# Layer 1 attention of a two-block kernel: score products issued as a set, the query norm's factor taken into the softmax, other order estimates

## The chip, the core and the metric

The kernel runs on one core of one Trainium2 chip. The metric is the device time of one execution in microseconds (us), taken as the median of repeated runs. The engines of the core are named as in the profile: PE is TensorE (PEld its weight loads), DVE is VectorE, ACT is ScalarE, POOL is GpSimd and SP is SyncE, which here issues the loads.

## What is computed

Two transformer blocks follow each other on 256 tokens of 1024 features, in float32. The first has dilated attention, a state-space part and a gated feed-forward. The second has two layers with a modulation from a conditioning vector: layer 0 is a convolution module on two streams (the latent x and a context), layer 1 is grouped-query attention of x over both streams. The change is in layer 1; this is its part of the reference, cut to what matters:

```python
def gqa_project(h, w_qkv, q_norm, k_norm):
    ...   # 16 query heads, 4 key heads, 64 wide
    return rms_norm(q, q_norm), rms_norm(k, k_norm), v

def softmax_attend(q, k, v):
    s = jnp.einsum('bkgqd,bkld->bkgql', q, k).astype(jnp.float32) * (q.shape[-1] ** -0.5)
    p = jax.nn.softmax(s, axis=-1).astype(v.dtype)
    return jnp.einsum('bkgql,bkld->bkgqd', p, v)

def gqa_mixer(hl, hc, w_qkv, q_norm, k_norm, w_o, tables, with_ctx):
    ...
    ql = apply_axial_rope(ql, tables)
    kl = apply_axial_rope(kl, tables)
    k_all = jnp.concatenate([kc, kl], axis=2)      # 512 keys
    ...
    ol = merge_heads(blocked_attend(ql, k_all, v_all)) @ w_o
```

`rms_norm` divides a head's 64 values by the root of their mean square and multiplies by a gain per value.

## The kernel before

**Recording and ordering.** The program does not issue its instructions as it goes. `Recorder.add` notes each of them with the tiles that it reads and writes and with a cost in nanoseconds from `Recorder.cost`. `Recorder.schedule` then plays the engines against each other with these costs: an engine that is free takes, of the instructions whose inputs are ready and whose tiles have room, the one that comes first in the program. The result is one fixed order for each engine, and that is what runs. So a changed cost moves instructions in the whole program, not only where the change was made. `together` puts several products into one entry of that list, so that nothing comes between them.

**Products in three passes.** Weights and activations are split into a high and a low part (names with h and l: `gh`, `gl`, `hqkv`, `lqkv`), and each product runs as low x high, high x high, high x low. ACT makes the high part, DVE the low one.

**Layer 1 attention.** `q_proj` computes eight tiles of two query heads each (products `pq`, 24 per tile, copied to `qf`) and their squares' sums (`hsq`); after four tiles `HeadNorm.done` works out 1/rms on [128 tokens, 16] tiles (`hn`, a chain of ten small DVE instructions). `q_norm(j)` calls `HeadNorm.apply`: four PE products `hb` (each shows as two records) spread the factor over the partitions, DVE multiplies `qf` by gain and factor (`ht`), then come the rotation (a shuffle, two products with the tables `cos2` and `sin2`, a sum) and the split to `q1h`, `q1l`. Keys go through the same function to `k1h`, `k1l`.

For each pair of heads j (8) and half of the queries i (2), called a unit below (16 units), there are two heads side by side. The scores of a head are three products `S` that use 64 of the array's 128 rows (form 64\*128 in the trace); the two heads sit in the two halves of the rows and can run side by side. DVE takes the row maximum (`am`), ACT the exponential (`P`, with its sum `dn`), DVE scales by 1/sum. PE transposes P in four pieces a head (`pt`, form 128\*128), ACT copies them (`PT`), and eight products `po` (form 128\*64, together in one set) give the output, split to `o1h`, `o1l`. The output projection `pw` follows; some of it runs between the units. Scores of the first half go to PSUM banks of tag `at`, those of the second to `py` and `sb`; transposes and `hb` share the bank `ax`, and from the second pair on one head's transposes use `md`.

**Other stages that the order touches.** The modulation of layer 0 is 24 groups of four products `pm` of form 128\*32, spread as fillers over the first part of the program. The state-space part ends in eight sets of products `py`, which need DVE's tiles `DF`. In the convolution of the latent stream DVE works through 152 taps (`lcv`); a chain of mean (`mul`), square sums (`sslb`), a small norm (`pclb`, `bclb`) and DVE's `lsl` ends in the products `p<-lsl`. The context's products there read `csl` and `csh`.

Of the kernel before, what the change touches and what calls it, by code (L numbers as in the profile page):

```python
# [21 lines left out]
T = 256  # L22
# [7 lines left out]
# ---------------------------------------------------------------------------  # L30
# Weight streams: each stream is a list of chunks; a chunk is [128, w] in SBUF.
# ---------------------------------------------------------------------------
# [21 lines left out]
# columns of the parameter pack  # L54
# [3 lines left out]
def _prm(spec):  # L58
# [9 lines left out]
    ("wdw", 248), ("bdw", 8), ("lng", 8), ("lnb", 8), ("gq", 1), ("gk", 1),  # L68
# [30 lines left out]
HURRY, C2, CS_TAG = 4, 2, "S"  # L99
UC = ("sE", "sE", "sw", "sw")  # L100
# [5 lines left out]
# ---------------------------------------------------------------------------  # L106
# Recording of the kernel's instructions, and a list scheduler that orders them.
# ---------------------------------------------------------------------------
def _rearranged(a, pattern, sizes):
    # numpy form of AP.rearrange for the few patterns used here  # L110
# [21 lines left out]
class View:  # L132
    """A part of a virtual tile: `ix` are the elements that it covers, in quadrants of 32 partitions."""
# [47 lines left out]
class Op:  # L181
    __slots__ = ("n", "eng", "calls", "outs", "deps", "cost", "lat", "prio", "succ", "wait", "reserve",
                 "tiles", "start", "end", "pos", "cols", "urgent", "begun", "ready")


class Section:
    """Instructions that `spread` sets between others of the program."""
# [17 lines left out]
class Recorder:  # L205
# [18 lines left out]
    @contextmanager  # L224
    def together(self, rounds):
        # instructions of one engine that stay together: products in column tiles that run side by side
        self.set = []
        yield
        parts, self.set = self.set, None
        op = parts[0]  # L230
        op.deps = sorted({d for o in parts for d in o.deps})
        op.calls = [c for o in parts for c in o.calls]
        op.outs = [v for o in parts for v in o.outs]
        op.tiles = list({id(t): t for o in parts for t in o.tiles}.values())
        one = max(o.cost for o in parts)
        op.cost = rounds * one + 25.0 * (len(parts) - rounds)
        op.cols = rounds * one * 2.4
        self.ops.append(op)
        self.prio += 1.0

    def add(self, eng, fn, args, kw):
# [36 lines left out]
        op.cost, op.lat = self.cost(eng, fn, args, kw, ins, outs)  # L278
        if eng == "tensor":
            op.cols = (op.cost - 2.5) * 2.4 * min(1.0, args[1].shape[0] / 128)  # L280
# [8 lines left out]
    def cost(self, eng, fn, args, kw, ins, outs):  # L289
        """Nanoseconds that an instruction holds its engine, and until others see its result."""  # L290
# [5 lines left out]
        if eng == "tensor":  # L296
            moving = args[2] if fn == "matmul" else args[1]
            n = math.prod(moving.shape[1:]) if fn == "matmul" else 128
            f32 = args[1].dt == FT
# [10 lines left out]
        if fn == "tensor_tensor_scan":  # L310
            return 100 + 1.042 * n, 140.0
# [15 lines left out]
    def schedule(self):  # L327
        """Orders the instructions: each engine takes, when it is free, the ready one that comes first in the program
        and whose tiles fit. Tiles are taken early only where all that comes before still fits."""
# [10 lines left out]
        # room left in each tag along the program  # L340
# [22 lines left out]
        columns = {}  # L363
        soon = {e: [] for e in engines}
        while done < len(ops):
            progress = False
            for e in engines:
# [39 lines left out]
                if e == "tensor":  # L407
                    # the array runs at half its rate until one tick of its clock's monitor was busy
                    tick_ = int(now / HAM_TICK)
                    if columns.get(tick_ - 1, 0.0) < HAM_COLUMNS:  # L410
                        cost = max(25.0, 2 * (cost - 2.5))
                    n = pick.cols
# [19 lines left out]
            while future and future[0][0] <= now:  # L432
                _, kind, _, n = heapq.heappop(future)
                op = ops[n]
                # its own engine sees a result at once, the others after `lat`
# [32 lines left out]
def two_blocks(ctx: ExitStack, tc: tile.TileContext, I, out):  # L468
# [15 lines left out]
    def held(mark):  # L484
        # not before the instruction of that mark
# [21 lines left out]
    class Feat:  # L507
        # n feature tiles of w columns each, in pieces of 4 KiB (tag S) or 3 KiB (tag Q)
# [100 lines left out]
    def rsqrt(v, y, t, h):  # L609
        # y = 1/sqrt(v) for v > 0: a guess from the bits, and a polynomial of v guess^2  # L610
# [12 lines left out]
    class Norm:  # L623
        # 1 / rms over the features of [128, 8, T] tiles; broadcast over partitions
# [16 lines left out]
        def column(self, pc):  # L641
            # the mean square of each token, tokens on partitions
# [14 lines left out]
    def spread_rows(y, n, name, tag="ax"):  # L657
        # [128 tokens, 2 n] -> [128, n, T], the same on every partition
# [8 lines left out]
    def two_rstd(n1, n2):  # L667
        # n1 for x, n2 for g x: 1 / rms(x) and its product with 1 / rms(g x / rms(x))
# [68 lines left out]
    # ======================= block 1 =========================================  # L737
# [25 lines left out]
    # SSM parameters and rotary tables of block 1  # L763
# [4 lines left out]
    ssc = const("ssc", [128, 16, 16], FT)  # small SSM vectors  # L768
# [8 lines left out]
    def prelude():  # L777
# [13 lines left out]
        # rotary tables: [token, (quadrant, half, freq)] transposed to [dim, token]  # L791
# [10 lines left out]
        # z = (abar - 1) / lambda  # L802
# [15 lines left out]
        # c' = c z  # L818
# [17 lines left out]
    # u = n @ w_in[u]  # L836
# [17 lines left out]
    def cmul(oc, os, ac, as_, bc_, bs, shape, name):  # L854
        # (oc + i os) = (ac + i as)(bc + i bs)
# [9 lines left out]
    def ssm():  # L865
        # tables e^{i theta t}, t = 16 a + b, from A[b] and B[a]
        # the rotation starts anew at each half of the sequence
        H = T // 2
        tabs = slot("tabs", [128, 2, 2, 16, 16])  # (cos/sin, A/B, n, state tile)
# [10 lines left out]
        for q in range(4):  # L880
            py = bank("py", (128, T), "py")
            E = [rec.tile("sE", [128, 4, 8, 16], FT, "E") for _ in range(2)]  # cos/sin: (state tile, a, b)
# [5 lines left out]
            for s2 in range(2):  # L888
                DF = []
                for s in (2 * s2, 2 * s2 + 1):  # L890
# [19 lines left out]
                    for h in range(2):  # L910
                        if h:
                            # the state in the new frame: e^{i theta 128} g
# [13 lines left out]
                # y = c're (D_re - F_im) - c'im (F_re + D_im)  # L926
# [52 lines left out]
    def mod_part(parts):  # L979
        # sixths of layer 1's modulation for a stream each: weighted on the vector engine, summed over partitions  # L980
        # on the tensor engine
# [32 lines left out]
    # chunks of the modulation: 0 shift1, 8 scale1, 16 gate1, 24 shift2, 32 scale2, 40 gate2  # L1014
    def modulated(x, gain, bias, bc, put, name):
        # put(k) -> (hi, lo) destinations
# [25 lines left out]
    def conv_front(hx, s, name, on_pe, tg, stag, ntag="ax"):  # L1042
        # convolution module from its modulated input up to the last product's operand
        st = Stream("pw1")
        acc = Feat(name + "cv")
        for j in range(8):
# [10 lines left out]
            # some taps as products with diagonal matrices, the others on the vector engine  # L1057
# [17 lines left out]
        # layer norm over features  # L1075
# [26 lines left out]
    def do_mods(groups, a, b):  # L1102
        # these groups of the modulation, between places a and b of the program
# [14 lines left out]
    def slot_proj(j):  # L1118
# [27 lines left out]
        vv = slot("vv", [128, 2, 384], FT, "Q")  # (token block, 3 heads x 128)  # L1146
# [4 lines left out]
    def slot_attn(j, q_, k_, vv):  # L1151
        sp = bank("sp", (128, 2, T), "at")  # scores of the third group, and the output
        po = sp[:, 1]
        for i in range(2):
# [20 lines left out]
            pt = slot("PT", [128, 3, nk], FT, "Q")  # (group, (key block, query))  # L1175
# [33 lines left out]
    def table(fn, mark):  # L1209
        # loads the tables of a function ahead of its first use  # L1210
# [561 lines left out]
```

## Time and profile before

| | |
|---|---|
| three runs | 1479.51, 1482.2, 1485.17 us; median 1482.2 us |
| the profiled execution, first to last instruction | 1482.9 us |
| PE busy | 1449.6 us (98%), 10324 matmul records |
| DVE busy | 1138.5 us (77%) |
| ACT busy | 739.4 us (50%) |
| mean granted TensorE clock | 0.989 of full speed |
| bytes read | 238.42 MB |

The three runs lie 0.2% around their median. Of the profiled execution only the span is known, 0.7 us above the median; nothing outside it is shown. A PE record's duration covers its way through the pipeline, so records overlap; what a product costs is read from one start to the next. A clock of 1.00 is 2.4 GHz and 0.50 is 1.2 GHz.

### The profile page before, as it was taken

The page shows a single profiled execution, that of the slowest core. Times are in us where ns is not written, and L with a number is a line of the kernel's source. Part 1 is how long each engine was busy: PE and PEld are TensorE (multiplying, and loading weights), DVE is VectorE, ACT ScalarE, POOL GpSimd, SP SyncE. Part 2 cuts the span into 40 slices and gives each one's busy share as a digit, 9 for nine tenths or more (in the row PEclk, how much of TensorE's full clock was granted, in tenths as well). Part 3 has the DMA queues.
Part 4 walks back from the last instruction along what each step waited for, and adds up shares of the span by engine and source line. Part 5 has one row for each costly group of instructions (what it writes and reads, how often), then busy time and mean ns, then how long its engine had stood idle before and what let it go on. Part 6 is the DMA issues. An engine that isn't in the chain of part 4 may idle for free.

```text
span 1482.9 us, 26349 instructions
## 1 busy us (share of the span) xinstructions
PE 1449.6 (98%) x10324; PEld 1290.1 (87%) x10324; DVE 1138.5 (77%) x2336; ACT 739.4 (50%) x1337; POOL 0.2 (0%) x4
## 2 busy tenths in 40 slices
PE   6999999999999999999799999999999999999999
PEld 5878779989999998798699787878788977899999
DVE  7899996779999998789778987564446669777643
ACT  4545455554444446566455334433334447677632
POOL 0000000000000000000000000000000000000000
PEclk9999999999999999999999999999999989999999
DMA  8753454675655565544145777552221420355663
GB/s 335 265 187 111 169 176 152 210 231 188 189 176 184 169 200 185 173 133 148 46 131 186 225 246 246 179 179 92 94 93 40 130 81 15 101 175 183 189 196 99
DMA packets 68524, 241.18 MB, mean 163 GB/s; under 512 B 7728, under 2 KB 9264, under 8 KB 68400
## 3 DMA queue, kind: packets, MB, share of 16 engines
q1 hardware_dynamic: 68400, 239.50, 50.0%
q8 instruction: 81, 1.33, 0.4%
q14 instruction: 43, 0.35, 0.1%
HBM read 238.42 MB, written 1.05 MB: 161 GB/s over the span
## 4 chain that ended last, share of the span: by engine, by line
PE 93%; DVE 4%; ACT 2%; DMA 1%; issue 0%; ACTq 0%; DVEq 0%
PE pf L464 37%; PE pq L464 7%; PE fg L464 4%; PE pd L464 4%; PE fu L464 4%; PE pa L464 3%; PE pv L464 3%; PE cvp L464 3%; PE pg L464 3%; PE p L464 3%; PE m L464 2%; PE pgt L464 2%; PE pw L464 2%; PE S L464 1%; PE pm L464 1%; PE pe L464 1%
## 5 line engine op out<-in xcount | busy, mean ns | idle before, releaser
L464 DVE TENSOR_TENSOR lffb<-rffb,hffb 128x1024 fp32r<-128x1024 f32 x64 | 78.4, 1225 | 87.1 <-ACT hffb L464 87.1
L464 ACT ACTIVATE hffb<-rffb 128x1024 fp32r<-128x1024 f32 x64 | 67.9, 1061 | 147.7 <-PE pf L464 145.0
L464 ACT ACTIVATE hffa<-rffa 128x1024 fp32r<-128x1024 f32 x64 | 68.0, 1062 | 119.7 <-PE pf L464 109.9
L464 DVE SCALAR_TENSOR_TENSOR ccv<-ucc,prm,ccv 128x241 f32<-128x241 f32 (+14 forms) x240 | 110.5, 474 | 2.1
L464 PE MATMUL pf<-eul,hffb 128*128 128x512 f32 (+1 forms) x288 | 107.2, 372 | 0.0
L464 PE MATMUL pf<-euh,lffb 128*128 128x512 f32 (+1 forms) x288 | 106.8, 371 | 0.0
L464 PE MATMUL pf<-euh,hffb 128*128 128x512 f32 (+1 forms) x288 | 106.5, 370 | 0.0
L464 PE MATMUL pf<-eh,hffa 128*128 128x512 f32 (+1 forms) x288 | 106.5, 370 | 0.0
L464 PE MATMUL pf<-el,hffa 128*128 128x512 f32 (+1 forms) x288 | 106.1, 370 | 0.0
L464 PE MATMUL pf<-eh,lffa 128*128 128x512 f32 (+1 forms) x288 | 106.1, 369 | 0.0
L464 DVE TENSOR_TENSOR lffa<-rffa,hffa 128x1024 fp32r<-128x1024 f32 x64 | 78.2, 1224 | 15.4 <-ACT hffa L464 15.0
L464 DVE SCALAR_TENSOR_TENSOR xT<-pf,mods,xT 128x256 f32<-128x256 f32 x72 | 34.8, 483 | 62.8 <-PE pf L464 62.5
L464 ACT ACTIVATE hgu<-rgu 128x1024 fp32r<-128x1024 f32 x44 | 46.4, 1059 | 69.5 <-PE fu L464 31.6
L464 ACT ACTIVATE hpw<-rpw 128x1024 fp32r<-128x1024 f32 x48 | 50.7, 1058 | 59.3 <-PE pa L464 10.5
L464 ACT ACTIVATE hqkv<-rqkv 128x1024 fp32r<-128x1024 f32 (+1 forms) x52 | 51.6, 994 | 54.5 <-PE pq L464 27.4
L464 DVE SCALAR_TENSOR_TENSOR ma<-rmod,cvec,ma 128x1024 f32<-128x1024 f32 x56 | 70.7, 1280 | 2.6 <-DMA rmod<-in_w_mod_dram 2.3
L464 PE MATMUL pf<-zh,hffa 128*128 128x258 f32 x256 | 72.4, 283 | 0.0
L464 PE MATMUL pf<-zl,hffa 128*128 128x258 f32 x256 | 72.3, 283 | 0.0
L464 PE MATMUL pf<-zh,lffa 128*128 128x258 f32 x256 | 72.3, 282 | 0.0
L464 PE MATMUL pf<-zuh,lffb 128*128 128x256 f32 x256 | 72.2, 282 | 0.0
L464 PE MATMUL pf<-zuh,hffb 128*128 128x256 f32 x256 | 72.1, 282 | 0.0
L464 PE MATMUL pf<-zul,hffb 128*128 128x256 f32 x256 | 72.0, 281 | 0.0
(565 smaller groups left out, 4974.1 us busy)
## 6 DMA issues: line engine op xcount, KB each, us to landing
rmod<-in_w_mod_dram SPq DMA_DIRECT2D x96, 512.0 KB, 4.3
rffa<-in_w_ffa_dram SPq DMA_DIRECT2D x64, 512.0 KB, 3.6
rffb<-in_w_ffb_dram SPq DMA_DIRECT2D x64, 512.0 KB, 3.6
rpw<-in_w_pw_dram SPq DMA_DIRECT2D x48, 512.0 KB, 4.1
rgu<-in_w_gu_dram SPq DMA_DIRECT2D x44, 512.0 KB, 3.6
rqkv<-in_w_qkv_dram SPq DMA_DIRECT2D x36, 512.0 KB, 4.3
rdown<-in_w_down_dram SPq DMA_DIRECT2D x22, 512.0 KB, 4.2
rgates<-in_w_gates_dram SPq DMA_DIRECT2D x16, 512.0 KB, 3.8
```

The lines of the kernel that those rows point to most:

```text
L464: getattr(getattr(self.nc, op.eng), fn)(*map(real, args), **{k: real(v) for k, v in kw.items()})
```

## The change

Three things are changed. The six score products of a unit become one entry of the list. The queries are no longer multiplied by their norm's factor: the gain goes into copies of the rotation's tables (multiplied in place once the keys have used them), the factor times 0.125 goes to the softmax as a scale per token (`rq`), and `hb` is issued for the keys alone. And three of the scheduler's costs are changed: products of split operands cost 5.6 ns and 0.4414 ns a column, a scan on DVE costs about twice as much, and a product whose form differs from that of the product before it costs 92 ns more.

```diff
@@ columns of the parameter pack
-    ("wdw", 248), ("bdw", 8), ("lng", 8), ("lnb", 8), ("gq", 1), ("gk", 1),
+    ("wdw", 248), ("bdw", 8), ("lng", 8), ("lnb", 8), ("gq", 1), ("gqs", 1), ("gk", 1),
...
+CHANGE = 92.0
@@ Recorder.add
+        op.form = None
         if eng == "tensor":
+            op.form = (args[1].shape[0], args[0].shape[0])
@@ Recorder.cost
+            if args[1].dt == FR:
+                return 5.6 + n * 0.4414, 200.0
             f32 = args[1].dt == FT
...
         if fn == "tensor_tensor_scan":
-            return 100 + 1.042 * n, 140.0
+            return (48 if isinstance(kw.get("initial"), float) else 108) + 2.083 * n, 140.0
@@ Recorder.schedule
+                    if pick.form != form:
+                        cost += CHANGE
+                    form = pick.form
@@ layer 1 attention
-    hq = []
+    rq = [small([128, 2, 8], tag="rq", n=2) for _ in range(2)]
...
         hn.done()
-        hq.append(hn)
+        ts(rq[kt], hn.r, 0.125, None, OP.mult)
...
+    qcos, qsin = cc("cos2"), cc("sin2")
+    ts(qcos, qcos, pp("gq"), None, OP.mult)
+    ts(qsin, qsin, pp("gqs"), None, OP.mult)
+
     def q_norm(j):
-        hq[j // 4].apply(j % 4, qf[j], pp("gq"), True, *q1[j])
+        t, sh = tmp("qt", (128, T)), tmp("qh", (128, T))
+        V.stream_shuffle(out=sh, in_=qf[j], mask=[i ^ 16 for i in range(32)])
+        tt(t, qf[j], qcos, OP.mult)
+        tt(sh, sh, qsin, OP.mult)
+        tt(t, t, sh, OP.add)
+        split(t, *q1[j])
...
-            for n_, (w_, x_) in enumerate(((qh, kl), (qh, kh), (ql, kh))):
-                for hf, S in enumerate(Ss):
-                    a = slice(64 * hf, 64 * hf + 64)
-                    PE.matmul(S, w_[a, qs], x_[a], start=n_ == 0, stop=n_ == 2, tile_position=(64 * hf, 0))
+            with rec.together(3):
+                for n_, (w_, x_) in enumerate(((qh, kl), (qh, kh), (ql, kh))):
+                    for hf, S in enumerate(Ss):
+                        a = slice(64 * hf, 64 * hf + 64)
+                        PE.matmul(S, w_[a, qs], x_[a], start=n_ == 0, stop=n_ == 2, tile_position=(64 * hf, 0))
             for hf, S in enumerate(Ss):
+                r = rq[j // 4][:, i, 2 * (j % 4) + hf:2 * (j % 4) + hf + 1]
...
-                ts(m[:, 1:2], m[:, 0:1], -0.125, None, OP.mult)
+                ts(m[:, 1:2], m[:, 0:1], r, -1.0, OP.mult, OP.mult)
...
-                A.activation(P, S, AF.Exp, bias=m[:, 1:2], scale=0.125, accum_out=dn[:, 0:1])
+                A.activation(P, S, AF.Exp, bias=m[:, 1:2], scale=r, accum_out=dn[:, 0:1])
```

In the built program PE loses 32 products (`hb` of the queries: 48 become 16), and everything else is moved. From the first score product to the last `po` the array changes its form 82 times before and 63 times now; over the whole program 240 and 226 times.

At PE's first scores, the order before has single score products between products of `pq`. A name's number is that of its buffer: S_2284 and S_2285 are the two heads of the first unit, S_2296 and S_2297 those of the second.

```order
L464 MATMUL S_2284_13097<-k1l_2174_12858,q1h_2167_13091 128x512
L464 MATMUL S_2285_13099<-k1l_2174_12858,q1h_2167_13091 128x512
L464 MATMUL S_2284_13097<-k1h_2173_12835,q1h_2167_13091 128x512
L464 MATMUL S_2285_13099<-k1h_2173_12835,q1h_2167_13091 128x512
L464 MATMUL pq_2251_13052<-gh_2101_12380,lqkv_2254_12937 128x256
L464 MATMUL S_2296_13108<-k1l_2174_12858,q1h_2167_13091 128x512
L464 MATMUL pq_2251_13052<-gl_2105_12396,hqkv_2253_12924 128x256
L464 MATMUL S_2284_13097<-k1h_2173_12835,q1l_2170_13103 128x512
L464 MATMUL S_2285_13099<-k1h_2173_12835,q1l_2170_13103 128x512
L464 MATMUL pq_2251_13052<-gh_2101_12380,hqkv_2253_12924 128x256
L464 MATMUL S_2297_13118<-k1l_2174_12858,q1h_2167_13091 128x512
L464 MATMUL pq_2251_13052<-gh_2101_12380,lqkv_2254_12937 128x256
```

At the same place, the first scores of the changed kernel:

```order
L473 MATMUL pq_2243_12981<-gh_2102_12419,hqkv_2245_12836 128x256
L473 MATMUL S_2282_13028<-k1l_2174_12838,q1h_2167_12920 128x512
L473 MATMUL S_2283_13029<-k1l_2174_12838,q1h_2167_12920 128x512
L473 MATMUL S_2282_13028<-k1h_2173_12822,q1h_2167_12920 128x512
L473 MATMUL S_2283_13029<-k1h_2173_12822,q1h_2167_12920 128x512
L473 MATMUL S_2282_13028<-k1h_2173_12822,q1l_2170_12928 128x512
L473 MATMUL S_2283_13029<-k1h_2173_12822,q1l_2170_12928 128x512
L473 MATMUL pq_2243_12981<-gh_2102_12419,lqkv_2246_12897 128x256
```

The six products now stand in a row, the two heads in turn; 40 products of `pq` follow before the second unit's scores. From the first score product to the last `po` there are now 73 products of `pq` and 22 of `pw`, where there were 34 and 37.

In the middle of the attention on PE, the order before has the heads' scores and transposes at changing places, with `hb` among them:

```order
L464 MATMUL po_2387_13690<-PT_2376_13636,v_2176_12647 64x128 x8
L464 MATMUL hb_13702<-cst_72,hn_13334 64x128 x4
L464 MATMUL pt_2401_13711<-cst_72,P_2399_13651 128x128 x4
L464 MATMUL S_2429_13719<-k1l_2174_12858,q1h_2168_13206 128x512
L464 MATMUL S_2429_13719<-k1h_2173_12835,q1h_2168_13206 128x512
L464 MATMUL S_2429_13719<-k1h_2173_12835,q1l_2171_13214 128x512
L464 MATMUL pt_2397_13726<-cst_72,P_2395_13620 128x128 x4
L464 MATMUL pt_2413_13733<-cst_72,P_2411_13687 128x128 x4
```

The changed kernel repeats one pattern there; this is one turn of it:

```order
L473 MATMUL S_2360_13430<-k1l_2174_12838,q1h_2168_13054 128x512
L473 MATMUL S_2361_13431<-k1l_2174_12838,q1h_2168_13054 128x512
L473 MATMUL S_2360_13430<-k1h_2173_12822,q1h_2168_13054 128x512
L473 MATMUL S_2361_13431<-k1h_2173_12822,q1h_2168_13054 128x512
L473 MATMUL S_2360_13430<-k1h_2173_12822,q1l_2171_13072 128x512
L473 MATMUL S_2361_13431<-k1h_2173_12822,q1l_2171_13072 128x512
L473 MATMUL pt_2339_13448<-cst_72,P_2337_13392 128x128
L473 MATMUL po_2330_13450<-PT_2319_13426,v_2176_12594 64x128 x8
L473 MATMUL pt_2339_13448<-cst_72,P_2337_13392 128x128 x3
L473 MATMUL pt_2343_13472<-cst_72,P_2341_13409 128x128 x4
```

A turn holds the scores of one unit, the transposes of the unit two before it (P_2337 and P_2341 come from scores issued two turns ahead) and the output products of the unit three before it.

On PE at the end of the latent convolution, the order before puts two products of the context (`csl`, `csh`) between the small norm's last product `bclb` and the first product that reads `lsl`:

```order
L464 MATMUL bclb_8978<-cst_72,nw_8969 128x128 x2
L464 MATMUL p_1538_8985<-csl_817_7313,hpw_1540_8974 128x256
L464 MATMUL p_1538_8985<-csh_815_7299,hpw_1540_8974 128x256
L464 MATMUL p_1598_9010<-lsl_1507_9005,hpw_1600_8515 128x256
L464 MATMUL p_1598_9010<-lsh_1504_8998,hpw_1600_8515 128x256
```

In the changed kernel the same place begins so:

```order
L473 MATMUL bclb_8978<-cst_72,nw_8966 128x128 x2
L473 MATMUL p_1538_8983<-csl_817_7193,hpw_1540_8973 128x256
L473 MATMUL p_1538_8983<-csh_815_7176,hpw_1540_8973 128x256
L473 MATMUL p_1538_8983<-csh_815_7176,lpw_1541_8985 128x256
L473 MATMUL p_1538_8983<-csl_817_7193,hpw_1540_8973 128x256
```

All 24 products of that tile stand there now, ahead of the first that reads `lsl`. The fillers `pm` moved too: of the 24 groups 12 stood before the first product of the block's mixing (`m`) and 20 before the latent convolution's input norm (`bcnf`); now it is 9 and 14, and ten of them, where there were four, stand between `bcnf` and `sslb`.

## Rows read from the trace of the kernel before

**Rows 1.** The span and clock of the core, and two lines of the page.

```profile
core 0: 1482.9 us, clock 0.989
...
PE 1449.6 (98%) x10324; PEld 1290.1 (87%) x10324; DVE 1138.5 (77%) x2336; ACT 739.4 (50%) x1337; POOL 0.2 (0%) x4
...
PE 93%; DVE 4%; ACT 2%; DMA 1%; issue 0%; ACTq 0%; DVEq 0%
```

**Rows 2.** Stretches: length; busy us (count) of PE, PEld, DVE, ACT, POOL; clock; DMA.

```profile
0.00:240.00 240.00, 226.12 (x1599) 189.47 (x1600) 221.51 (x592) 122.92 (x256) 0.20 (x4) 0.99 0.60 205
610.00:700.00 90.00, 88.39 (x599) 79.22 (x600) 82.05 (x181) 54.78 (x113) 0.00 (x0) 0.98 0.38 131
1198.00:1276.00 78.00, 77.09 (x619) 56.80 (x618) 60.39 (x208) 49.09 (x130) 0.00 (x0) 0.91 0.07 22
1202.00:1215.00 13.00, 12.52 (x47) 9.47 (x48) 6.87 (x23) 4.16 (x14) 0.00 (x0) 0.50 0.00 0
1210.00:1215.00 5.00, 5.00 (x25) 5.00 (x25) 3.37 (x12) 1.70 (x10) 0.00 (x0) 0.50 0.00 0
1220.00:1255.00 35.00, 34.77 (x314) 25.41 (x315) 33.47 (x123) 26.53 (x71) 0.00 (x0) 1.00 0.02 5
1300.00:1400.00 100.00, 100.00 (x838) 99.94 (x837) 71.97 (x131) 75.96 (x132) 0.00 (x0) 1.00 0.59 180
```

**Rows 3.** PE in order of time at the first scores: start us, us, what.

```profile
1198.95 0.50 PE L464 MATMUL S<-k1l,q1h 64*128 64x512 f32 x2
...
1199.61 0.39 PE L464 MATMUL pq<-gh,lqkv 128*128 128x256 f32 x1
1199.93 0.49 PE L464 MATMUL S<-k1l,q1h 64*128 64x512 f32 x1
1200.35 0.38 PE L464 MATMUL pq<-gl,hqkv 128*128 128x256 f32 x1
```

**Rows 4.** PE in order of time in the middle of the attention.

```profile
1231.50 0.49 PE L464 MATMUL S<-k1l,q1h 64*128 64x512 f32 x1
...
1232.38 1.09 PE L464 MATMUL po<-PT,v 128*64 128x128 f32 x16
1233.31 0.61 PE L464 MATMUL hb<-cst,hn 128*64 128x128 f32 x8
1233.85 0.51 PE L464 MATMUL S<-k1l,q1h 64*128 64x512 f32 x2
1234.19 0.40 PE L464 MATMUL S<-k1h,q1h 64*128 64x512 f32 x2
1234.42 0.40 PE L464 MATMUL S<-k1h,q1l 64*128 64x512 f32 x2
1234.75 1.09 PE L464 MATMUL pt<-cst,P 128*128 128x128 f32 x8
1235.60 0.36 PE L464 MATMUL pw<-o1l,hwo 128*128 128x256 f32 x1
```

**Rows 5.** PE in order of time, later in the attention and at its end.

```profile
1263.64 0.66 PE L464 MATMUL pt<-cst,P 128*128 128x128 f32 x4
1264.23 1.09 PE L464 MATMUL po<-PT,v 128*64 128x128 f32 x16
1265.26 0.44 PE L464 MATMUL pt<-cst,P 128*128 128x128 f32 x2
...
1275.02 0.39 PE L464 MATMUL pw<-o1h,hwo 128*128 128x256 f32 x1
```

**Rows 6.** Groups of instructions, 1198 to 1276 us: count, busy us, mean ns, idle before.

```profile
L464 DVE SCALAR_TENSOR_TENSOR ht<-qf,prm,hb 128x256 f32<-128x256 f32 x6 | 2.9, 475 | 0.7 <-PE hb L464 0.7
...
L464 ACT ACTIVATE P<-S,am 128x512 f32<-128x512 f32 x32 | 21.9, 691 | 0.5 <-DVE hn L464 0.4
```

**Rows 7.** PE in order of time in the latent convolution.

```profile
661.44 1.06 PE L464 MATMUL pm<-rmod,cvec 128*32 128x512 f32 x8
...
739.98 0.39 PE L464 MATMUL p<-lsl,hpw 128*128 128x256 f32 x1 [2.32 <-DVE lsl L464]
```

More of the change, by code (lines that the diff above doesn't have):

```diff
@@ L182 @@
     __slots__ = ("n", "eng", "calls", "outs", "deps", "cost", "lat", "prio", "succ", "wait", "reserve",
-                 "tiles", "start", "end", "pos", "cols", "urgent", "begun", "ready")
+                 "tiles", "start", "end", "pos", "cols", "urgent", "begun", "ready", "form")
 class Section:
@@ L362, in schedule @@
         order, now, tick, front, done = [], 0.0, 0, 0, 0
-        columns = {}
+        columns, form = {}, None
         soon = {e: [] for e in engines}
@@ L1685, in _params @@
     put("gq", np.tile(i["gqa_q_norm_2"][0], 2))
+    put("gqs", np.tile(i["gqa_q_norm_2"][0][np.arange(64) ^ 16], 2))
     put("gk", np.tile(i["gqa_k_norm_2"][0], 2))
```

## The prediction, made before the changed kernel ran

> **What bounds the kernel now.** The first view is the page's busy shares and the chain that ended last: PE is busy 98% of the 1482.9 us and makes up 93% of the chain, so time is won where PE's own starts come closer together, and lost where another engine makes it wait [rows 1]. The second is the table of stretches. Where only dense three-pass products run, PE starts 838 of them in 100 us, 0.119 us each [rows 2]; nothing in the change touches those. The reader should compare that with the attention: from the first score product at 1198.95 to the first product after the last `po` at 1275.02 [rows 3, 5], 76.1 us, the clock averages 0.91, because for 13 us it stood at 0.50, which is 1.2 GHz [rows 2]. What PE did before it fell is in the third view, PE in order of time: single score products alternate with single `pq` products. A `pq` between two scores takes 0.32 us from start to start, 0.20 more than in the dense stretch, and a lone score 0.42 [rows 3]. In the middle of the attention the clock is 1.00, PE has no visible gap, and DVE is busy 33.5 of 35 us [rows 2]: it is nearly as full as PE.
>
> **The change part by part: the attention.** I rebuild the stretch from start-to-start prices at 2.4 GHz. Six score products in pairs, with the change of form behind them, take 0.90 us (1233.85 to 1234.75); three alone take 0.88 (1231.50 to 1232.38), so pairing makes the second head free [rows 4]. A set of `po` with the change behind it takes 1.03 us (1264.23 to 1265.26) [rows 5], 0.93 without (1232.38 to 1233.31) [rows 4]. Eight transposes take 0.85, so a head's four 0.43 [rows 4]; with a change of form behind them 0.59 (1263.64 to 1264.23) [rows 5], so a change costs 0.16. A set of `hsq` has no row here; I take it like four transposes, 0.43.
>
> The changed order has, from its first score to the first product after its last `po`: 16 sixes 14.4 us; 16 `po` 16.5; 32 heads of transposes 13.6; 21 changes behind transposes 3.4; 95 `pq` and `pw` at 0.119, 11.3; 9 changes behind those, taken at 0.16, 1.4; four `hsq` 1.7. Sum 62.3 us. The order before has 24 `pq` and `pw` (2.9 us) and two `hsq` (0.9) fewer there, so on equal work it took 76.1 + 3.8 = 79.9. That is 17.6 us. Three of the eight removed `hb` stand ahead of the stretch, each 0.54 us (1233.31 to 1233.85) [rows 4] and one more change, 0.70: 2.1 us. Upper end of the gain: 19.7 us. It contains the clock: with scores in sixes and 12 and 28 `pq` between the first ones, the mixture that stood ahead of the fall is gone.
>
> The lower end comes from DVE. It is busy 60.4 us in the stretch [rows 2]. Removed are the multiplications `ht` of the query tiles, 0.475 each, six of them inside [rows 6]: 2.9 us. Added are two products with the tables, two small `rq`, a pointer in the 32 small `am`: together about 1.5 us at most by the same row. So DVE needs 59 us. At its densest share, 33.5 of 35, that is 61.7 us, and it cannot fill the ends: ahead of the first maximum and behind the last one, where PE alone still has six heads of transposes, four `po` and 17 `pw` (9.5 us by the prices above), it stands idle some 5 or 6 us. DVE alone would give about 67.5 us, and the gain would be 79.9 - 67.5 + 2.1 = 14.5. ACT is busy 49.1 us of the stretch [rows 2]. What a second pointer costs the exponential no row shows; below it is nothing, above I take a quarter of its 691 ns [rows 6], 5.5 us over 32, and 54.6 still lies under 62.3: hidden, at most late by the quarter in the chain of a unit, which has two turns of some 3.1 us of PE work until its transposes. Between 14.5 and 19.7 I take 17: PE's sum is the longest of the three once the early work has passed, but three engines this full will not interlock without some waits.
>
> **The change part by part: everything else.** The dense stretches keep their work. What moves is the filler `pm`, about 1 us a group [rows 7]. Six groups leave the part ahead of the latent convolution and come into it. Three of them leave the first 240 us, where DVE is busy 221.5 us [rows 2]: if `py` only waits there for `DF`, nothing is won, if not 3 us; I take 1. Three leave the part between, where PE is the bound: 3 us won. In the convolution PE is busy 88.4 of 90 us and DVE 82.1 [rows 2], so six groups cost up to 6 us and, if DVE is late anyway, nothing; I take 6, as PE is the fuller. Behind `bclb` PE waited 2.32 us for `lsl` [rows 7]; 22 more products stand ahead of that read, 2.6 us, so I take the wait as gone. Sum: -1 - 3 + 6 - 2.3 = -0.3. The other exchanges of neighbours I cost at nothing, since they move dense products against dense products; ends for all of this: -8.3 (3 and 3 won, `pm` free in the convolution, the wait gone) and +3 (nothing won in the first 240 us, the wait still there), and another 3 us for exchanges around the scans.
>
> **Sum.** 1482.9 - 17 - 0.3 = 1465.6 us. The profiled execution lies 0.7 us above the median of the runs; I leave that in. The measurement can tell about 0.5%, 7.4 us, from no change, so faster means below 1474.8.
>
> **The rivals.**
> 1. *DVE sets the pace of the attention, and each unit's transposes wait for the scaled P.* For it: DVE's 33.5 of 35 us in the middle. Against it: part of that were query norms, of which most now fall among the `pq` products ahead of the turns. The stretch would be 67.5 us or a little more: 14.5 us won, less about 1 for interlocking: 1469.
> 2. *The moved fillers are lost.* PE comes to `py` sooner, waits for `DF`, and later pays for the groups in the convolution, where each brings two changes of form as well. For it: DVE's 92% in the first 240 us. Against it: PE waits 2.32 us and more at the convolution's end, which the moved work can fill. Price +6 on the rest: 1472.
> 3. *Slower: the clock stays at 1.2 GHz through the turns of the attention.* In the cold stretch 25 products took 5 us [rows 2], 0.20 instead of 0.119, a factor of 1.7. Sixteen turns are 49 us of PE time by the prices above, so all of them cold add 34 us: 1500. It decides from 17.3 / 0.7 = 25 us of half clock on, against the 13 us that the stretch had before. Against it: 35 us with transposes, scores and `po` in the mix ran at 1.00 [rows 2], and a turn has fewer changes of form than that. The Trainium skill, page "TensorE: Matmul & The Clock Gate", section "Part 4: PE-mode transpose", says that a transpose does not count as engine activity for the clock gate as other products do. By that rule a pattern that is a good quarter transposes would be the one to fall; the 35 us at 1.00 do not agree with it as far as this kernel goes.
> 4. *The pairs do not run side by side.* Then a six costs twice 0.88 [rows 4], 13.8 us more in all: 1479. Rows 4 show pairs that do, so this has little.
>
> **How the numbers follow.** Forecast 0.60, DVE's pace 0.18, fillers lost 0.14, low clock 0.06, no pairing 0.02. Likeliest: 1465.6. The range runs from 1457 (upper end of the attention, most of the rest's) to 1477 (fillers lost, with the 3 us for the scans and a little more); it leaves out the low clock, the missing pairs and about a tenth of the others. Faster by over 0.5%: nearly all of the forecast (0.59), most of DVE's pace (0.16), over half of the lost fillers (0.08): 0.83. Slower by over 0.5%: the low clock, 0.06. Within: 0.11.
>
> **What the changed profile would show.** Right: about 62 to 67 us from the first `S` to the first product after the last `po`, sixes with 0.90 from start to start, turns of about 3.1 us, the clock at 1.00 from the first score on, 16 `hb` products; the wait ahead of `p<-lsl` gone. Wrong in the attention's price: turns of 3.5 us or more, with PE waiting for P or for PT; DVE above 95% busy in them would be rival 1. Wrong in the rest: waits of PE ahead of `py`, and `bcnf` no earlier than before with `pa` later, would be rival 2; a stretch at 0.50 rival 3. The prediction fails most easily if the first 760 us gain or lose more than 6 us by exchanges that I costed at nothing.

## The result, and the profile after

The changed kernel takes 1465.11 us (median of 4 runs, 1464.0 to 1465.94); the kernel before took 1480.99 us beside it (median of 4). The ratio on record is 0.9883, interval 0.9866 to 0.9901, which is 17.3 us; it is not the quotient of these two medians, 0.9893, which lies inside the interval. The profiled execution spans 1463.6 us, 19.3 less than that of before. First the page's span of the core with its clock, the busy time of each engine and the chain that ended last, which answer to [rows 1]:

```profile
core 0: 1463.6 us, clock 0.994
...
PE 1432.5 (98%) x10260; PEld 1277.6 (87%) x10260; DVE 1140.4 (78%) x2332; ACT 741.3 (51%) x1337; POOL 0.2 (0%) x4
...
PE 93%; DVE 4%; ACT 1%; DMA 1%; issue 1%; SPq 0%; ACTq 0%
```

PE is as full as before and has 17.1 us less to do, so the time went out of PE's own work (which counts the 13 us at 0.50 of before as busy), not out of its idle time. The table of stretches says where (columns as in [rows 2]):

```profile
0.00:240.00 240.00, 226.09 (x1619) 191.84 (x1620) 223.35 (x598) 125.82 (x263) 0.20 (x4) 1.00 0.58 194
610.00:700.00 90.00, 89.67 (x602) 77.60 (x602) 80.22 (x165) 54.90 (x115) 0.00 (x0) 0.98 0.51 171
1191.00:1256.00 65.00, 64.98 (x608) 50.88 (x608) 57.26 (x204) 53.62 (x134) 0.00 (x0) 1.00 0.15 49
1215.00:1240.00 25.00, 25.00 (x245) 18.11 (x243) 24.28 (x86) 22.71 (x58) 0.00 (x0) 1.00 0.08 23
```

The attention is the third and fourth row: the clock is 1.00 throughout, PE has no gap, DVE is busy 24.28 of 25 us in the turns and ACT 22.71. Below is PE in order of time at the first score, for one turn and the beginning of the next, and at the end of the attention; it answers to [rows 3 to 5]:

```profile
1191.65 0.50 PE L473 MATMUL S<-k1l,q1h 64*128 64x512 f32 x2
...
1216.06 0.50 PE L473 MATMUL S<-k1l,q1h 64*128 64x512 f32 x2
1216.39 0.39 PE L473 MATMUL S<-k1h,q1h 64*128 64x512 f32 x2
1216.62 0.40 PE L473 MATMUL S<-k1h,q1l 64*128 64x512 f32 x2
1216.95 0.33 PE L473 MATMUL pt<-cst,P 128*128 128x128 f32 x1
1217.21 1.09 PE L473 MATMUL po<-PT,v 128*64 128x128 f32 x16
1218.23 0.98 PE L473 MATMUL pt<-cst,P 128*128 128x128 f32 x7
1219.15 0.51 PE L473 MATMUL S<-k1l,q1h 64*128 64x512 f32 x2
...
1254.65 0.39 PE L473 MATMUL pw<-o1h,hwo 128*128 128x256 f32 x1
```

From the first score to the first product after the last `po` it is 63.0 us (1191.65 to 1254.65), where it was 76.1 with 24 `pq` and `pw` fewer. A six takes 0.89, a turn 3.09. The milestones of PE put the rest in order: the last `py` starts 12.35 us sooner than before (225.28), the block's first mixing product 5.4 sooner, `bcnf` 4.3 sooner, `bclb` 1.1 later, the first `hb` 0.4 later (1172.60 against 1172.23), and the last product 19.3 sooner (1459.96 against 1479.24). So in these two executions everything ahead of the attention cancels out, and from the first `hb` to the end PE takes 287.4 us instead of 307.0: 19.6 us less.

The groups of ACT and DVE in the attention that got a second pointer (columns as in [rows 6]):

```profile
L473 ACT ACTIVATE P<-S,am,rq 128x512 f32<-128x512 f32 x32 | 24.8, 785 | 1.1 <-DVE am L473 1.1
...
L473 DVE TENSOR_SCALAR am<-am,rq 128x1 f32<-128x1 f32 x32 | 5.5, 200 | 0.0
```

And PE at the end of the latent convolution, with the wait in brackets, which answers to [rows 7]. The first product that reads `lsl` waits no more, but there is a new wait for the split of a weight (`lpw`) in the products that were set ahead of it:

```profile
739.79 0.39 PE L473 MATMUL p<-csh,lpw 128*128 128x256 f32 x1 [0.76 <-DVE lpw L473]
...
742.51 0.28 PE L473 MATMUL p<-lsl,hpw 128*128 128x256 f32 x1
```

### The profile page after: what moved, and what is told of

Its sections match the earlier page's. It is cut to its first block, busy times and chain, and to the rows that moved or that the text cites. A ratio compares the mean times of both kernels' runs of the same rounds, so it can differ in the third digit from the quotient of the medians.

```text
span 1463.6 us, 26274 instructions
## 1 busy us (share of the span) xinstructions
PE 1432.5 (98%) x10260; PEld 1277.6 (87%) x10260; DVE 1140.4 (78%) x2332; ACT 741.3 (51%) x1337; POOL 0.2 (0%) x4
## 4 chain that ended last, share of the span: by engine, by line
PE 93%; DVE 4%; ACT 1%; DMA 1%; issue 1%; SPq 0%; ACTq 0%
PE pf L473 37%; PE pq L473 6%; PE fg L473 4%; PE pd L473 4%; PE fu L473 4%; PE pgt L473 3%; PE cvp L473 3%; PE p L473 3%; PE pg L473 3%; PE pa L473 3%; PE pv L473 3%; PE m L473 2%; PE pe L473 2%; PE pw L473 2%; PE pm L473 1%; PE pt L473 1%
## 5 line engine op out<-in xcount | busy, mean ns | idle before, releaser
L473 DVE TENSOR_TENSOR lffb<-rffb,hffb 128x1024 fp32r<-128x1024 f32 x64 | 78.4, 1225 | 88.2 <-ACT hffb L473 88.2
L473 DVE SCALAR_TENSOR_TENSOR ccv<-ucc,prm,ccv 128x241 f32<-128x241 f32 (+14 forms) x240 | 113.8, 474 | 4.6 <-ACT ccv L473 0.5
L473 DVE TENSOR_TENSOR lffa<-rffa,hffa 128x1024 fp32r<-128x1024 f32 x64 | 78.2, 1224 | 19.8 <-ACT hffa L473 19.3
L473 DVE SCALAR_TENSOR_TENSOR lcv<-ucl,prm,lcv 128x241 f32<-128x241 f32 (+9 forms) x152 | 67.9, 471 | 10.4 <-ACT lcv L473 7.5
```

Of the source, the lines that this page charges most:

```text
L473: getattr(getattr(self.nc, op.eng), fn)(*map(real, args), **{k: real(v) for k, v in kw.items()})
```

## The experiments

**The change in parts.** Four kernels hold one or two of its three parts. The stretch "first `hb` to the end" is given for each, since what lies ahead of it differs by up to 9 us between executions even where the order is the same (last section). Times and ratios are against the kernel before as it ran beside them, with medians of 1482.96 (e1 to e4), 1481.87 (e5 to e8) and 1482.7 us (e9 to e12).

*Only the estimates* (to the kernel before):

```diff
+CHANGE = 92.0
...
+            if args[1].dt == FR:
+                return 5.6 + n * 0.4414, 200.0
...
-            return 100 + 1.042 * n, 140.0
+            return (48 if isinstance(kw.get("initial"), float) else 108) + 2.083 * n, 140.0
...
+                    if pick.form != form:
+                        cost += CHANGE
```

> Only the three estimates of the scheduler are changed; scores are loose and hb is kept. Theory 1 (the whole gain comes from the attention's PE starts; the estimates move dense products against dense products and trade waits): within 3 us of the kernel before, ratio 0.998 to 1.002, and a stretch of 10 us or more at a granted clock of 0.50 after the first score, as before. Theory 2 (the estimates win time by filling waits, in the first 240 us and behind the latent convolution): 4 to 8 us faster, ratio 0.995 or less.

Measured 1483.51 us, ratio 1.0001 (0.9986 to 1.0017). Up to the attention the profile shows what the changed kernel's shows (last `py` 11.8 us sooner than before, first `hb` 0.1 later), and in the attention the low clock of before. Its stretch of 10 us from 1203, columns as in [rows 2]:

```profile
1203.00:1213.00 10.00, 10.00 (x35) 7.11 (x36) 7.47 (x22) 5.88 (x15) 0.00 (x0) 0.58 0.17 50
```

By themselves the estimates bring nothing: theory 1.

*Only the set* (to the kernel before):

```diff
+            with rec.together(3):
+                for n_, (w_, x_) in enumerate(((qh, kl), (qh, kh), (ql, kh))):
...
```

> Only the six score products of a unit are issued as a set; estimates and norm as before. Theory 1 (start-to-start sum): pairing, fewer changes of form and the clock, without the eight hb of 0.70 us each: 17 - 5.6 = 11 to 12 us faster, ratio 0.992, sixes of 0.90 us, clock 1.00 from the first score to the last po. Rival (DVE sets the pace, with the query norms' work still in the turns): 6 to 8 us faster, ratio 0.995, with PE waiting in front of pt or S. Rival (the low clock comes from the query norms and single hb, not from mixed scores): a stretch at 0.50 remains, 5 us faster or less.

Measured 1477.35 us, ratio 0.9955 (0.9938 to 0.9972); from the first `hb` 298.1 us, 8.9 less than before. The clock stays at 1.00, but PE has gaps and DVE has none. The turns, and what PE waited for from 1200 to 1266 (us in all, times, longest):

```profile
1205.00:1235.00 30.00, 26.14 (x240) 19.01 (x238) 29.17 (x104) 21.67 (x57) 0.00 (x0) 1.00 0.13 37
```
```profile
PE pt L471 <- DVE P L471: 2.0, 3, 1.2
```

This wait for the scaled `P` is about half of PE's waits there (3.8 us); the others are for `PT` and `P` of ACT. With DVE busy 29.17 of 30 us this fits the second theory, DVE as the pace, in the kernel that still has the query norms' work in the turns. My 11 to 12 us were wrong for this kernel.

*Only the norm* (to the kernel before, the diff's lines on `rq`, `qcos`, `qsin`, `q_norm` and the two scales):

```diff
-        hq[j // 4].apply(j % 4, qf[j], pp("gq"), True, *q1[j])
...
+        tt(t, qf[j], qcos, OP.mult)
+        tt(sh, sh, qsin, OP.mult)
...
+                A.activation(P, S, AF.Exp, bias=m[:, 1:2], scale=r, accum_out=dn[:, 0:1])
```

> Only the query norm's factor is moved; scores are loose, estimates as before. Theory 1: eight hb sets of 0.70 us less, 5 to 6 us faster, ratio 0.996, with the clock still falling to 0.50 where single scores stand between pq products. If the clock stays at 1.00 with loose scores, then the fall was not due to the mixture, and 10 us or more are won, ratio 0.993 or less.

Measured 1478.29 us, ratio 0.9964 (0.9949 to 0.9979); from the first `hb` 298.3 us, 8.7 less. The time agrees with theory 1, its condition doesn't: the scores are loose (36 groups; 30 in the kernel before, 16 sets in the changed one), single ones stand between `pq` products, and the clock holds:

```profile
1194.00:1210.00 16.00, 16.00 (x94) 11.74 (x93) 11.79 (x43) 8.35 (x19) 0.00 (x0) 1.00 0.23 67
```

So loose scores alone did not make it fall in this execution. Without `hb`, two `pq` stand between two scores here where it was one in [rows 3].

*Set and norm, old estimates* (to the changed kernel):

```diff
-CHANGE = 92.0
+CHANGE = 0.0
...
-            if args[1].dt == FR:
-                return 5.6 + n * 0.4414, 200.0
...
-            return (48 if isinstance(kw.get("initial"), float) else 108) + 2.083 * n, 140.0
+            return 100 + 1.042 * n, 140.0
```

> Set and norm as in the changed kernel, all three estimates as before. Theory 1: the time of the changed kernel within 2 us, 1464 to 1467, ratio 0.987 to 0.990. Theory 2 (the estimates bring part of the gain): 1469 or more, ratio 0.992 or more. Should the old order be the better one (it has 57 changes of form in the attention where the changed kernel has 62, five times 0.16 us, and loses nothing in the convolution): 1463 or less.

Measured 1468.91 us, ratio 0.9900 (0.9883 to 0.9917). The interval overlaps that of the changed kernel, so the time leaves it open. The trace has 289.7 us from the first `hb` on, 2.3 more than the changed kernel, and waits of PE in the attention that the changed kernel has not:

```profile
PE S L471 <- ACT P L471: 0.8, 2, 0.5
PE pt L471 <- ACT PT L471: 0.8, 1, 0.8
```

In number the two parts add up (8.9 and 8.7 to 17.3). But each of their profiles also lacks the 13 us at 0.50 that the profile of before has, and this gain, some 5 us by an estimate in the next section, can be counted only once. That leaves about 12 for the parts and some 5 that only come with both, which fits a DVE that holds the sixes back until the norm's work has left it; no run shows this by itself. The times lean the same way (0.45% and 0.36% against 1.00%), within their intervals. The estimates may give some 2 us on top, in the attention itself and only there.

**What a six costs.** Both kernels are the changed one, with the issue order touched inside the attention alone, after the scheduling. First the heads in turn within a set:

```diff
+            if name.startswith("S1_"):
+                calls = calls[0::2] + calls[1::2]
```

> The changed kernel with one thing different: within each set of six, the three products of one head come first, then those of the other; all else keeps its place. Theory 1 (a six costs 0.90 us because products of the two row halves run side by side when they alternate, and three alone cost 0.88): each set takes about 1.76 us, 16 sets 13.8 us more, 1479 us, ratio 0.997, if DVE, now with less to do per turn, adds nothing. Rival (side by side or not, DVE sets the pace): under 5 us more, ratio 0.992 or less.

Measured 1465.92 us, ratio 0.9893 (0.9874 to 0.9912): no difference, and not the 13.8 us more of theory 1. In the profile the products of the two heads still stand in pairs, though three of one head were issued ahead of three of the other:

```profile
1212.10 0.51 PE L476 MATMUL S<-k1l,q1h 64*128 64x512 f32 x2
1212.44 0.40 PE L476 MATMUL S<-k1h,q1h 64*128 64x512 f32 x2
1212.67 0.40 PE L476 MATMUL S<-k1h,q1l 64*128 64x512 f32 x2
1213.01 0.33 PE L476 MATMUL pt<-cst,P 128*128 128x128 f32 x1
```

So the order in which a set is issued is not what pays; what puts the products side by side all the same, no run shows. Then a transpose between the heads:

```diff
+            if op.outs and op.outs[0].tile.name.startswith("S1_"):
+                other = Op()
+                other.eng, other.outs, other.calls = "tensor", [], op.calls[1::2]
+                op.calls, late = op.calls[0::2], other
+            elif op.eng == "tensor" and late:
+                order.append(late)
...
```

> The changed kernel with the three products of a unit's second head one PE entry later, so that (in the turns) a single transpose stands between the two heads; nothing else is moved. Theory 1 (two heads side by side in 0.90 us, a head alone 0.88): a turn takes 0.86 us more and one change of form, 14 to 16 us in all, ratio 0.998. Rival (adjacency is worth only the changes of form): 16 times 0.16, under 3 us, ratio 0.990.

Its twelve runs lie in two groups: seven from 1479.41 to 1484.11 us at a mean clock of 0.993 to 0.997, and five from 1489.49 to 1495.2 at 0.983 to 0.987 (median of all 1483.17, ratio 1.0023, 0.9998 to 1.0048; the second group lifts it above the 0.998 that I expected). The profiled execution is of the second group, and shows both prices. One turn at the clock of 1.00:

```profile
1260.79 0.49 PE L483 MATMUL S<-k1l,q1h 64*128 64x512 f32 x1
1261.12 0.39 PE L483 MATMUL S<-k1h,q1h 64*128 64x512 f32 x1
1261.36 0.39 PE L483 MATMUL S<-k1h,q1l 64*128 64x512 f32 x1
1261.67 0.33 PE L483 MATMUL pt<-cst,P 128*128 128x128 f32 x1
1261.93 0.50 PE L483 MATMUL S<-k1l,q1h 64*128 64x512 f32 x1
1262.27 0.39 PE L483 MATMUL S<-k1h,q1h 64*128 64x512 f32 x1
1262.51 0.39 PE L483 MATMUL S<-k1h,q1l 64*128 64x512 f32 x1
1262.83 1.09 PE L483 MATMUL po<-PT,v 128*64 128x128 f32 x16
```

Each head alone takes 0.88 to 0.90 us up to the next form, the turn 3.98 (1260.79 to 1264.77) instead of 3.09: 0.89 more, 14.2 in 16 units. The middle of the first group is 1481.3, some 16 us above the changed kernel. Theory 1 holds: the second head is free when nothing stands between the two, whatever the order in which the set is issued; the rival's price, 0.16 a unit, is far from 0.89. And the low clock came, for 32 us:

```profile
1216.00:1248.00 32.00, 32.00 (x141) 21.91 (x139) 16.34 (x61) 14.29 (x35) 0.00 (x0) 0.50 0.00 1
```

**Who sets the pace of the turns.** Five kernels are the changed one with some work more or less in the attention; everything else keeps its place. The stretch from the first score to the first product after the last `po` is read as above (63.0 us in the changed kernel). The lines that pick the instructions are left out here. What the kernels leave out: e6 and e11 half of the multiplication by 1/sum, e10 and e11 the third pass of the scores, e12 the norm's factor.

```diff
 # e6: half of each P scaled
+                calls = [(fn, (args[0][:, 0:256], args[1][:, 0:256], *args[2:]), kw) for fn, args, kw in calls]
 # e7: am <- am, rq twice
+                calls = calls * 2
 # e10: four products in a set, the last pass left out; e11: e10 and e6
+                calls = [(fn, args, dict(kw, stop=i >= 2)) for i, (fn, args, kw) in enumerate(calls[:4])]
 # e12: in P and in am
+                calls = [(fn, args, dict(kw, scale=0.125)) for fn, args, kw in calls]
```

> The changed kernel with only the first half of each P multiplied by 1/sum in layer 1 (the other half is left as it is), everything in its place. By the 478 ns row that takes some 0.2 us of 32 instructions, 6.4 us of DVE. Theory 1 (PE's starts set the pace of the turns, DVE is just fast enough): within 1 us of the changed kernel, ratio 0.987 to 0.990. Rival (DVE sets the pace): 4 to 6 us faster than the changed kernel, ratio 0.985 or less.

> The changed kernel with the small product am <- am, rq issued twice in each head, 32 instructions of 200 ns more on DVE, everything else in its place. Theory 1 (DVE just fast enough: 24.3 us busy in 25 in the turns, the rest of its idle time at the ends): most of the 6.4 us shows, 4 to 6 us more than the changed kernel, 1469 to 1471, ratio 0.992. Rival (PE has the bound alone and DVE has room): 1 us or less, ratio 0.989.

> The changed kernel without the third pass (low query times high key) of the scores in layer 1: four products in a set where there were six, one pair of 0.23 us less in each of 16 units, 3.7 us less work for PE, everything else in its place. Theory 1 as it stands after the runs with less and more work for DVE (in the turns PE and DVE are equally long, each takes the pace as soon as the other is shorter): under 1.5 us faster than the changed kernel, ratio 0.987 to 0.989. Rival (PE alone sets the pace): 3.7 us faster, ratio 0.986 or less.

> The changed kernel without the third pass of the scores in layer 1, and with only the first half of each P multiplied by 1/sum: 3.7 us less for PE and some 6 us less for DVE. Theory 1 (PE and DVE equally long): the PE part shows now, 3 to 4 us faster than the changed kernel in the stretch, ratio 0.986, where each edit alone gives under 1.5. Rival (ACT or the chain of a unit comes next): under 1.5 us again.

| | stretch, us | time, us | ratio to before (interval) |
|---|---|---|---|
| changed kernel | 63.0 | 1465.11 | 0.9883 (0.9866 to 0.9901) |
| e6, less DVE | 62.9 | 1465.68 | 0.9894 (0.9877 to 0.9912) |
| e7, more DVE | 69.75 | 1474.17 | 0.9951 (0.9933 to 0.9969) |
| e10, less PE | 61.75 | 1464.63 | 0.9882 (0.9863 to 0.9900) |
| e11, less of both | 59.8 | 1464.32 | 0.9863 (0.9842 to 0.9884) |

The turns of e6, e7 and e10 in the table of stretches (PE's busy time is the third number, DVE's the fifth):

```profile
1215.00:1235.00 20.00, 19.98 (x199) 14.58 (x197) 19.31 (x78) 18.71 (x47) 0.00 (x0) 1.00 0.11 28
```
```profile
1215.00:1235.00 20.00, 18.24 (x172) 12.88 (x170) 19.64 (x76) 16.07 (x42) 0.00 (x0) 1.00 0.09 27
```
```profile
1215.00:1235.00 20.00, 19.31 (x183) 13.56 (x183) 20.00 (x72) 18.30 (x46) 0.00 (x0) 1.00 0.08 27
```

In e6 a scaling of `P` takes 346 ns instead of 478, so 4.2 us are off DVE (I had expected 6.4); PE is full and DVE idles a little: nothing is won. In e7 `am` takes 12.4 us in all instead of 5.5, and the stretch grows by 6.75 us, nearly all of the 6.9; its time lies 9 us above the changed kernel's, beyond my 4 to 6. In e10 DVE is full and PE has gaps: of 3.7 us only 1.25 shows. With both eased (e11) 3.2 us shows. PE and DVE are about equally long in the turns; there is little room on either. The times carry this only for e7, the differences of the others being below what they resolve; it rests on the stretches.

> The changed kernel with the constant 0.125 in place of the norm's factor, in the exponential and in am of layer 1 (the factor is left out of the result), everything in its place. Theory 1 (the exponential's 785 ns against 691 before is the price of the second pointer, and ACT hides it): exponentials back at about 690 ns, the time within 1 us of the changed kernel, ratio 0.987 to 0.989. Rival (ACT's later end delays DVE's reciprocal and so the pace): 2 to 3 us faster than the changed kernel, ratio 0.9865 or less.

Measured 1467.12 us, ratio 0.9890 (0.9872 to 0.9908); the stretch is 62.8 us. The exponential is back at 693 ns:

```profile
L478 ACT ACTIVATE P<-S,am 128x512 f32<-128x512 f32 x32 | 21.8, 693 | 0.7 <-DVE am L478 0.7
```

So the second pointer costs 92 ns an exponential, 3 us in all, and ACT hides them.

**A set for the transposes as well**, scheduled anew:

```diff
+                with rec.together(4):
                     for kb in range(4):
                         PE.transpose(tp[:, kb], P[:, 128 * kb:128 * kb + 128], ident)
```

> The changed kernel with the four transposes of a head issued as one set too, and scheduled anew with the same estimates. In the attention 53 changes of form instead of 62. Theory 1 (PE's starts set the pace, a change costs 0.16 us): 1.4 us faster than the changed kernel, 1463.7, ratio 0.987. Rival (DVE sets the pace): no difference, ratio 0.988; or slower by 1 to 3 us, if output products must wait for a whole set of transposes and DVE's work comes later.

Measured 1465.23 us, ratio 0.9885 (0.9867 to 0.9903), the stretch 62.3 us with five `pw` more and four `pq` fewer in it. Of the 1.4 us of theory 1 the stretch shows about half, the time nothing that it can tell, so the two theories are not told apart here and it is no better version.

## Why the prediction was right

**The sum for PE held.** 62.3 us were rebuilt from start-to-start prices, 63.0 were measured; six, `po` and transposes cost what [rows 4, 5] said. The reason given for the six, that pairing makes the second head free, stood the test of e9.

**The lower end from DVE was too careful.** It took 0.957 as the densest that DVE can run, and 14.5 us as the gain. In the changed kernel DVE runs at 24.28 of 25, and from 1215 to 1225 without a gap, while PE waits for nothing. The sign that I had set for the first rival, DVE above 95% busy in the turns, was there (97%), with turns of 3.09 us: by itself it tells nothing. So the gain from the first `hb` on was 19.6 us, at the upper end of 19.7 and not at the 17 that I took: that term was mis-sized by 2.6 us. DVE was nevertheless as near as the first rival had it: e2 ran at DVE's pace, and e7 shows that 6.9 us more on DVE cost 6.75. The added `am` cost 60 ns each, 1.9 us, where I had 1.5 for all that was added.

**The clock was right in its outcome, and wrong in its cause.** I put the fall to 0.50 down to single scores between single `pq`. e3 has single scores among `pq` at 1.00, and in e9 the clock fell behind some 4 us of scores, transposes and `hsq` without a `pq`. What brings the fall stays open. In the attention it stands in the profiles of the kernel before, e1 and e9, where one head's scores are mixed with other short work; e3 has such a mixture too and no fall, and no other profile has one there. How much of the gain it is, no run shows by itself. An estimate: by the factor 1.7 of the third rival the 13 us at 0.50 would have taken 7.6 at 1.00, so some 5 of the 19.6 us between the two profiles are the clock's. Over 50 executions of the kernel before the time follows the mean clock, 1485.7 us on average in the five at 0.989, 1480.1 in the nine at 0.994, which is the changed kernel's clock. Against those nine the change is worth some 15.0 us, about 2 less than the ratio gives. But a mean does not say where the clock was low: the changed kernel has 0.994 too, with 1.00 in the attention.

**The rest was right as a sum, not in its terms.** Forecast -0.3, measured +0.4, and 1.0001 for the estimates alone. But up to the first mixing product 5.4 us were won where I took 1, the part up to `bcnf` lost 1.1 where I took 3 won, and the convolution lost 5.4, near my 6. The wait for `lsl` went as forecast, yet from `bclb` to that product it takes 4.63 us instead of 3.24 for 22 products (2.6 us) more, so 1.2 us were won and not 2.3: the wait for `lpw` (0.76) took most of the remainder. All of this is read from one execution of each. In ten profiles with the changed order up to the attention (e1, e5 to e12 and the changed kernel) the first mixing product starts from 252.1 to 256.9 us and the convolution takes 129.0 to 130.7, in the four with the old order 257.2 to 261.0 and 125.1 to 126.4: these two are clear. The first `hb` starts from 1168.6 to 1177.8 in the ten and 1172.1 to 1177.1 in the four, so +0.4 in all cannot be told from my -0.3 or from a few us either way.

**The rivals.** The lost fillers (1472) are how the estimates' gain ahead of the attention went, except that the gain was larger than I took it to be. The low clock in the turns (1500) did not happen, but it was closer than 0.06 says: one transpose between the heads brings it in five executions of twelve (one by its trace, the others by their mean clock), to 1489.5 to 1495.2. That a transpose does not count for the clock gate as other products do (the Trainium skill, page "TensorE: Matmul & The Clock Gate", section "Part 4: PE-mode transpose") does not explain it, since the turns of the changed kernel hold the same eight transposes in less time and run at 1.00. The pairs ran side by side.

The sum, -19.6 + 0.4 = -19.2 on the span, was forecast as -17.3; the times moved by 15.9 us from median to median and 17.3 by the ratio. That 1465.6 came within 0.5 us of the measured 1465.11 is in part luck: the sum starts from a span, and times lie 1.8 us above spans (1465.4 and 1463.6 for the profiled execution of the changed kernel). As a span, 1465.6 is 2.0 too many, most of it the term of the attention.

## What to carry to other kernels

Where products of two row halves of the array can run side by side, keep everything else out from between them: one small transpose between them cost 0.89 us a unit, the order in which the set was issued nothing. When two engines are both near full, price an edit on both: taking work from PE alone gave 1.25 of 3.7 us, from DVE alone 0.1 of 4.2, from both 3.2; and the set alone ran into DVE while the norm's work was still there. A gain ahead of the stretch that sets the end is no gain until it is followed through: 12 us at `py` were none at the attention. And before the gains of two parts are added, ask whether both count the same thing, here the fall of the clock.

## What the runs showed of the hardware

The second pointer of an ACT instruction cost 92 to 94 ns at 128x512 (785 against 691 and 693). The Trainium skill, page "ScalarE: Activation LUTs", section "What ACT_TABLE_LOAD costs", gives about 93 ns for each such operand; the trace agrees, and it would have been the better source than the quarter that I took as an upper end. On DVE the pointer in `am` cost 60 ns (200 against 140).

Executions of one order differ by the clock in stretches far from any change. The same products `p` at the end of the convolution, in the kernel before and in e2 (start, us, what):

```profile
723.55 0.28 PE L464 MATMUL p<-csl,hpw 128*128 128x256 f32 x1
723.67 0.28 PE L464 MATMUL p<-csh,hpw 128*128 128x256 f32 x1
```
```profile
723.43 0.41 PE L471 MATMUL p<-csl,hpw 128*128 128x256 f32 x1
723.64 0.41 PE L471 MATMUL p<-csh,hpw 128*128 128x256 f32 x1
```

0.12 us from start to start in one, 0.21 in the other. PE's order is the same up to the first `hb` in the kernel before, e2, e3 and e4, and the first `hb` starts at 1172.2, 1172.1, 1176.0 and 1177.1. Of the kernels with the changed order it starts soonest in e5 (1168.6, mean clock 0.999) and latest in e7 (1177.8, 0.992). That is why small differences between kernels are better read from a stretch at one clock than from two spans.
